# Attention parts made two chunks ahead, and the second head's softmax one step behind the first's

## The chip, the cores and the metric

The kernel runs on one core of a Trainium2 chip. The metric is the device time of one execution in microseconds (us). The core has a matrix engine (TensorE, PE in the profile; its weight loads are PEld), a vector engine (VectorE, DVE), a scalar engine (ScalarE, ACT), a general engine (GpSimd, POOL) and a queue that issues most transfers (SyncE, SP). Each works through its own instructions in order and waits for the others by semaphores.

## The reference

A trunk of two layers over 256 tokens and 2048 features, in float32. The first layer mixes tokens by a gated MLP, the second by attention with a forget gate; each is followed by a convolutional feed-forward part. The change lies in the second layer's attention: 16 heads of 128 features, two blocks of 128 queries, the second of which sees all 256 keys.

```python
def forgetting_attention(xn, w_qg, q_norm, w_out, k, v, c):
    qg = xn @ w_qg
    q, g = jnp.split(qg, 2, axis=-1)
    q = rmsnorm(q.reshape(B, S, N_HEADS, HEAD_DIM), q_norm).transpose(0, 2, 1, 3)
    ...
        s = (jnp.einsum('bhqd,bhkd->bhqk', qb, kb).astype(jnp.float32) * scale
             + c[:, :, lo:hi, None] - c[:, :, None, :hi])
        mask = (lo + jnp.arange(Q_BLOCK))[:, None] >= jnp.arange(hi)[None, :]
        s = jnp.where(mask, s, -jnp.inf)
        p = jax.nn.softmax(s, axis=-1).astype(vb.dtype)
        outs.append(jnp.einsum('bhqk,bhkd->bhqd', p, vb))
    ...
    o = o * jax.nn.sigmoid(g)
    return o @ w_out
```

The keys k, the values v and the sums c of log forget gates come from one shared projection `w_kvf` of the first layer's output.

## The kernel before

**Chunks.** All projections are a single stream of weight chunks (class `Stream`), each 128 x 1024 numbers. For chunk i the loop in `run` issues the load of chunk i+6 on SP (L78, `raw`), splits chunk i+3 into a rounded part on ACT (L112, `whi`) and a remainder on DVE (L113, `wlo`), and then issues chunk i's matmuls (L216): rounded times rounded, rounded times remainder, remainder times rounded. There are four buffers each of `raw`, `whi` and `wlo`. In the values' blocks a chunk is 24 matmuls of 256 columns, and a block of 512 outputs has 8 chunks; in the gate's blocks (`b_g`) there are 4 chunks to a block of 256 outputs.

**Steps.** Everything that is not a weight matmul is written as generators. After each chunk's matmuls `advance` takes every pending generator one step further, to its next `yield`. So a `yield` is a distance of one chunk, and what stands between two of them is issued behind the chunk's matmuls, in the order in which the generators were started. Since ACT and DVE split three chunks ahead, their instructions for a step stand behind the split of the chunk three later.

**Attention.** `heads` is one of these generators. It starts with the first of the 32 chunks of the values (`kvf_v`) and runs on into the gate's chunks. It takes the heads in pairs, a pair every four chunks. A pass of its loop, which this text calls a batch, does this:

- the bias of the next pair's scores from `cB` and `ccol` on ACT (L1205, L1206), its mask on POOL (L1208), the fetch of the next `cB` rows (L1138, a transfer that POOL issues);
- on PE, the outputs of a pair whose weights are ready (`parts_pv`, and L1226), into a tile of the `ps` buffers, and the scores of the next pair (`parts_qk`, and L1229), into the two `mp` buffers;
- a `softmax` started for each of the two heads, and the outputs copied over their queries on ACT (L1233).

A product of the batch with 256 columns is made of parts as the weights' are: `query_parts` rounds queries and keys on ACT (L1166, L1167) and makes the remainders on DVE (L1169, L1170) a step later; `weight_parts` does the same for values and softmax weights (L1180, L1181, then L1185, L1188). There is one tile of parts for each of the two kinds, so they can be overwritten only when the batch before has read them.

`softmax` takes a head's scores from its `mp` buffer (L1147 on DVE, with the maximum in L1149), then exponentiates on ACT (L1152), then normalises and transposes on DVE (L1154, L1156, L953), a step each. `exchange` writes the transposed weights to memory in four transfers on SP (L960), and reads them back two steps later in another layout (L964). A step after that they are in `waiting`, from which `weight_parts` takes them.

Where `heads` starts, `head_norm` of the last block of keys still has work on DVE (L1048, L953). `between` lets the next weight matmuls run 512 columns wide. The buffers `ps` (three), `mp` (two), `big` (six) and `turned` (two) are given out as they come free.

Of the kernel before, what the change touches and what calls it, by code (L numbers as in the profile page):

```python
# [23 lines left out]
NH = 16  # L24
# [154 lines left out]
def build(ctx, tc, d, out):  # L179
# [25 lines left out]
    def main_ps():  # L205
        return psum.tile([P, 2, 512], F32, name="ps", tag="ps", bufs=3)

    def misc_ps():
        return psum.tile([P, 512], F32, name="mp", tag="mp", bufs=2)
# [5 lines left out]
    def mm(o, a, b, start, stop):  # L215
        nc.tensor.matmul(o, a, b, start=start, stop=stop, skip_group_check=True)  # L216

    def between():


        state["wide"] = [8, 2]
# [720 lines left out]
    def att(key):  # L942
        ph.open("att")
        shape = {"X2": [P, KD, 2 * T], "q": [P, NH, T], "k": [P, 4, 8, 4, 32], "v": [P, 2, D],
                 "ccol": [P, 2, NH], "gain": [P, 1]}[key]
        return ph.keep(key, shape, F32R if key == "X2" else F32)

    def blocks_turned(src):


        n = src.shape[1]
        turned = ph.temp("turned", [P, 512], bufs=1 if ph.name == "ffn1" else 2)[:, :n * P].rearrange("p (c h j) -> p c h j", c=4, h=n)
        nc.vector.transpose(turned.rearrange("p c h j -> p h c j"), src.rearrange("p h (c i) -> p h c i", c=4))  # L953
        return turned.rearrange("p c h j -> p c (h j)")
# [11 lines left out]
    def exchange(key, turned, new, then):  # L966

        way = rows_out(key, turned)
        yield
        yield  # L970
        dst = new()
        rows_in(dst, way)
        yield
        then(dst)
# [26 lines left out]
    def part_places(which):  # L1001

        side.open("parts")
        return [side.keep(f"{which}{n}", [P, 2, 2, n], F32R) for n in (P, T)]
# [56 lines left out]
    def four_rows(n):  # L1061
        return ph.temp("rows", [P, 512], bufs=6)[:, :n * P].rearrange("p (r x) -> p r x", r=4)
# [66 lines left out]
    def heads():  # L1129

        assert state["kept"]
        q, k, v, ccol = att("q"), att("k"), att("v"), att("ccol")
        rows, waiting, ready = {}, [], []
        (qp, kp), (vp, pp) = part_places("qk"), part_places("pv")

        def fetch(hd):
            rows[hd] = ph.temp("cB", [P, T])
            nc.gpsimd.dma_start(rows[hd], cd[hd:hd + 1, :].to_broadcast([P, T]))  # L1138

        def softmax(hd, S, L):  # L1140
            if hd % 2:
                yield
                yield
            parts = [(0, L[:, :P]), (1, L[:, P:])]
            mx = ph.temp("mx", [P, 2])
            sm = ph.temp("sm", [P, 2])
            nc.vector.scalar_tensor_tensor(L, S, SCALE, L, op0=OP.mult, op1=OP.add)  # L1147
            for tb, l in parts:
                nc.vector.tensor_reduce(mx[:, tb:tb + 1], l, axis=AX.X, op=OP.max, negate=True)  # L1149
            yield  # L1150
            for tb, l in parts:
                nc.scalar.activation(l, l, AF.Exp, bias=mx[:, tb:tb + 1], accum_out=sm[:, tb:tb + 1])  # L1152
            yield
            nc.vector.reciprocal(sm, sm)  # L1154
            for tb, l in parts:
                nc.vector.tensor_scalar(l, l, sm[:, tb:tb + 1], None, op0=OP.mult)  # L1156
            turned = blocks_turned(L.rearrange("p (h x) -> p h x", h=3))
            yield
            yield from exchange(f"p{hd}", turned, lambda: four_rows(3),
                                lambda dst: waiting.append((hd, dst.rearrange("p r (b j) -> p r b j", b=3))))  # L1160

        def query_parts(n):

            qq, kk = q[:, n:n + 2, P:], k[:, n // 4, :, n % 4:n % 4 + 2, :].rearrange("p t h j -> p h t j")
            kv = [kp[:, i].rearrange("p h (t j) -> p h t j", t=8) for i in range(2)]
            nc.scalar.activation(qp[:, 0], qq, AF.Copy)  # L1166
            nc.scalar.activation(kv[0], kk, AF.Copy)  # L1167
            yield
            nc.vector.tensor_tensor(qp[:, 1], qq, qp[:, 0].bitcast(F32), op=OP.subtract)  # L1169
            nc.vector.tensor_tensor(kv[1], kk, kv[0].bitcast(F32), op=OP.subtract)  # L1170

        def weight_parts():

            take = [hd for hd, _ in waiting if hd < state["v"]][:2]
            for hd in take:
                pT = waiting.pop(0)[1]
                i = hd % 2
                assert all(i != x % 2 for x, _ in ready)
                ready.append((hd, pT))
                nc.scalar.activation(vp[:, 0, i], v[:, 0, hd * P:(hd + 1) * P], AF.Copy)  # L1180
                nc.scalar.activation(pp[:, 0, i].rearrange("p (b r j) -> p r b j", b=2, r=4), pT[:, :, :2, :], AF.Copy)  # L1181
            yield
            for hd, pT in ready[len(ready) - len(take):]:
                i = hd % 2
                nc.vector.tensor_tensor(vp[:, 1, i], v[:, 0, hd * P:(hd + 1) * P], vp[:, 0, i].bitcast(F32),  # L1185
                                        op=OP.subtract)
                hi, lo = (pp[:, l, i].rearrange("p (b r j) -> p r b j", b=2, r=4) for l in range(2))
                nc.vector.tensor_tensor(lo, pT[:, :, :2, :], hi.bitcast(F32), op=OP.subtract)  # L1188

        def three(o, stat, mov, start, stop):  # L1190
            for j, (x, y) in enumerate(((0, 0), (0, 1), (1, 0))):
                mm(o, stat[:, x], mov[:, y], start and j == 0, stop and j == 2)

        for hd in range(2):
            fetch(hd)
        yield
        yield from query_parts(0)
        yield
        n = 0
        while state["done"] < NH:  # L1200
            pair = {hd: ph.temp("big", [P, 512], bufs=6)[:, :3 * P] for hd in (n, n + 1)} if n < NH else {}
            for hd, L in pair.items():
                cB = rows.pop(hd)
                l = L.rearrange("p (a b) -> p a b", a=3)
                nc.scalar.activation(l[:, 0, :], cB[:, :P], AF.Identity, scale=-1.0, bias=ccol[:, 0, hd:hd + 1])  # L1205
                nc.scalar.activation(l[:, 1:, :], cB.rearrange("p (a b) -> p a b", a=2), AF.Identity, scale=-1.0,  # L1206
                                     bias=ccol[:, 1, hd:hd + 1])
                nc.gpsimd.affine_select(l[:, 0::2, :], l[:, 0::2, :], pattern=[[0, 2], [-1, P]],  # L1208
                                        compare_op=OP.is_ge, fill=NEG, base=0, channel_multiplier=1)
                if hd + 2 < NH:  # L1210
                    fetch(hd + 2)
            if not pair and len(ready) < min(2, NH - state["done"]):
                yield from weight_parts()
                yield
                continue
            go, ready[:] = ready[:], []
            if go or pair:
                between()
            o = main_ps()[:, 0, :] if go else None
            S = {hd: misc_ps()[:, :3 * P] for hd in pair}  # L1220
            for i, (hd, pT) in enumerate(go):
                three(o[:, i * T:(i + 1) * T], vp[:, :, hd % 2], pp[:, :, hd % 2], i == 0, False)
            for hd in pair:
                three(S[hd][:, P:], qp[:, :, hd % 2], kp[:, :, hd % 2], True, False)
            for i, (hd, pT) in enumerate(go):
                nc.tensor.matmul(o[:, i * T + P:(i + 1) * T], v[:, 1, hd * P:(hd + 1) * P], pT[:, :, 2, :],  # L1226
                                 start=False, stop=True, skip_group_check=True)
            for hd, L in pair.items():
                nc.tensor.matmul(S[hd][:, :P], q[:, hd, :P], k[:, hd // 4, :4, hd % 4, :], start=False, stop=True,  # L1229
                                 skip_group_check=True)  # L1230
                s.start(softmax(hd, S[hd], L))
            for i, (hd, pT) in enumerate(go):
                nc.scalar.activation(q[:, hd, :], o[:, i * T:(i + 1) * T], AF.Copy)  # L1233
                state["done"] += 1
            yield
            if n + 2 < NH:
                yield from query_parts(n + 2)
            else:
                yield
            yield from weight_parts()  # L1240
            yield
            n += 2
        s.start(taken_back())
# [144 lines left out]
```

## Time and profile before

| | |
|---|---|
| median of 3 runs | 2169.18 us (2169.12 to 2170.85) |
| profiled execution | 2172.16 us, span 2170.4 us |
| PE busy | 2156.1 us, 99% of the span |
| DVE busy | 1648.4 us, 76% |
| ACT busy | 1212.9 us, 56% |
| granted TensorE clock, mean | 0.998 |
| first to last start of a score product of the batches | 1174.7 to 1273.0 us |

A row of the timeline gives start, duration, engine, line and operation, then output<-inputs; what follows in square brackets is the idle time of the engine ahead of it and what ended it. `att_big` is a `big` tile (here the scores), `att_X` the keys' and values' operand. In the stretches of the span, each engine's busy time is followed by its number of instructions, and the column after POOL is the granted clock as a share of full speed.

### The profile page before, as it was taken

The page shows a single profiled execution, that of the slowest core. Times are in us where ns is not written, and L with a number is a line of the kernel's source. Part 1 is how long each engine was busy: PE and PEld are TensorE (multiplying, and loading weights), DVE is VectorE, ACT ScalarE, POOL GpSimd, SP SyncE. Part 2 cuts the span into 40 slices and gives each one's busy share as a digit, 9 for nine tenths or more (in the row PEclk, how much of TensorE's full clock was granted, in tenths as well). Part 3 has the DMA queues.
Part 4 walks back from the last instruction along what each step waited for, and adds up shares of the span by engine and source line. Part 5 has one row for each costly group of instructions (what it writes and reads, how often), then busy time and mean ns, then how long its engine had stood idle before and what let it go on. Part 6 is the DMA issues. An engine that isn't in the chain of part 4 may idle for free.

```text
span 2170.4 us, 45367 instructions
## 1 busy us (share of the span) xinstructions
PE 2156.1 (99%) x18572; PEld 2138.7 (99%) x18572; DVE 1648.4 (76%) x2410; ACT 1212.9 (56%) x1692; POOL 25.4 (1%) x46
## 2 busy tenths in 40 slices
PE   9999999999999999999999999999999999999998
PEld 9999999999999999999999999999999999999998
DVE  6696687777777699976777886677877777779997
ACT  6665555555555555554545775455555555555555
POOL 0000000000000000000001100000000000000000
PEclk9999999999999999999999999999999999999999
DMA  8686566666666567776787877666866666666665
GB/s 310 189 242 206 193 198 194 191 197 190 198 193 195 178 201 224 225 227 193 250 251 257 237 220 236 194 215 190 270 194 194 192 197 191 197 192 186 205 204 165
DMA packets 159858, 454.68 MB, mean 209 GB/s; under 512 B 26321, under 2 KB 48609, under 8 KB 159265
## 3 DMA queue, kind: packets, MB, share of 16 engines
q1 hardware_dynamic: 158112, 447.82, 66.2%
q0 software_dynamic: 1072, 3.41, 0.6%
q8 instruction: 145, 2.38, 0.4%
q10 hardware_dynamic: 464, 0.55, 0.1%
q14 instruction: 65, 0.52, 0.1%
HBM read 434.39 MB, written 17.32 MB: 208 GB/s over the span
## 4 chain that ended last, share of the span: by engine, by line
PE 91%; DVE 4%; DMA 3%; issue 1%; ACT 1%; SPq 1%; DVEq 0%; POOL 0%; ACTq 0%; POOLq 0%
PE ps L216 89%; DVE wlo L113 2%; PE mp L216 1%; DMA way_h<-ffn_turned 1%; DMA raw<-kvf_v 1%; DMA raw<-kvf_k 1%; SPq L960 0%; ACT whi L112 0%; DVE att_big L1048 0%; DVE ffn_turned L953 0%; PE mp L780 0%; DMA way_k<-att_turned 0%; DMA raw<-b_g 0%; DMA raw<-kvf_fk 0%; PE mp L1229 0%
## 5 line engine op out<-in xcount | busy, mean ns | idle before, releaser
L113 DVE TENSOR_TENSOR wlo<-raw,whi 128x1024 fp32r<-128x1024 f32 (+1 forms) x732 | 888.1, 1219 | 282.4 <-ACT whi L112 278.0
L112 ACT ACTIVATE whi<-raw 128x1024 fp32r<-128x1024 f32 (+1 forms) x732 | 769.8, 1058 | 579.5 <-PE ps L216 451.8
L216 PE MATMUL ps<-X,whi 128*128 128x256 f32 (+1 forms) x6466 | 823.6, 280 | 0.0
L216 PEld LDWEIGHTS ps<-X,whi 128*128 128x128 f32 x6466 | 775.3, 188 | 6.8
L216 PE MATMUL ps<-X,wlo 128*128 128x256 f32 x3328 | 445.3, 276 | 0.2 <-DVE wlo L113 0.2
L216 PEld LDWEIGHTS ps<-X,wlo 128*128 128x128 f32 x3328 | 409.8, 188 | 2.1 <-DVE wlo L113 0.4
L216 PE MATMUL ps<-whi,ffn_H 128*128 128x256 f32 (+1 forms) x1852 | 303.1, 277 | 0.0
L216 PEld LDWEIGHTS ps<-whi,ffn_H 128*128 128x128 f32 x1852 | 255.5, 188 | 0.7
L216 PE MATMUL ps<-whi,X 128*128 128x256 f32 (+1 forms) x1336 | 221.9, 279 | 0.0
L216 PE MATMUL ps<-wlo,ffn_H 128*128 128x256 f32 (+1 forms) x924 | 192.3, 277 | 0.0
L216 PEld LDWEIGHTS ps<-whi,X 128*128 128x128 f32 x1336 | 187.7, 188 | 1.5
L924 DVE SCALAR_TENSOR_TENSOR ffn_room<-ffn_room,col 128x255 f32<-128x255 f32 x352 | 161.9, 481 | 6.4
L216 PE MATMUL ps<-whi,att_X 128*128 128x256 f32 (+2 forms) x970 | 164.3, 285 | 0.0
L216 PEld LDWEIGHTS ps<-wlo,ffn_H 128*128 128x128 f32 x924 | 144.4, 188 | 0.2
L216 PE MATMUL ps<-wlo,X 128*128 128x256 f32 (+1 forms) x666 | 144.4, 279 | 0.0
L216 PEld LDWEIGHTS ps<-whi,att_X 128*128 128x128 f32 x970 | 135.9, 188 | 3.4
L392 DVE TENSOR_TENSOR ffn_room<-ps,rB 128x512 f32<-128x512 f32 x76 | 52.5, 691 | 112.8 <-PE ps L216 112.8
L920 ACT ACTIVATE ffn_room<-ffn_room,col 128x256 f32<-128x256 f32 x176 | 96.3, 595 | 52.9 <-DVE ffn_room L392 52.9
L216 PEld LDWEIGHTS ps<-wlo,X 128*128 128x128 f32 x666 | 106.4, 188 | 0.4
L216 PE MATMUL ps<-wlo,att_X 128*128 128x256 f32 (+2 forms) x476 | 106.0, 287 | 0.0
L216 PEld LDWEIGHTS ps<-wlo,att_X 128*128 128x128 f32 x476 | 75.7, 188 | 1.1 <-DVE wlo L113 0.2
L90 ACT ACTIVATE whi<-raw 128x768 fp32r<-128x768 f32 x46 | 39.0, 848 | 65.0 <-PE ps L216 48.9
(229 smaller groups left out, 1696.1 us busy)
## 6 DMA issues: line engine op xcount, KB each, us to landing
raw<-up SPq DMA_DIRECT2D x352, 512.0 KB, 4.1
raw<-down SPq DMA_DIRECT2D x154, 512.0 KB, 4.3
raw<-a_in_u SPq DMA_DIRECT2D x32, 512.0 KB, 4.5
raw<-a_out SPq DMA_DIRECT2D x32, 512.0 KB, 4.0
raw<-b_q SPq DMA_DIRECT2D x32, 512.0 KB, 4.7
raw<-kvf_v SPq DMA_DIRECT2D x32, 512.0 KB, 4.6
raw<-b_g SPq DMA_DIRECT2D x32, 512.0 KB, 4.5
raw<-b_out SPq DMA_DIRECT2D x32, 512.0 KB, 4.3
```

Source lines behind the costliest of these rows:

```text
L90: self.nc.scalar.activation(hi[:, cols], src[:, cols], AF.Copy)
L112: self.nc.scalar.activation(h, raw, AF.Copy)
L113: self.nc.vector.tensor_tensor(l, raw, h.bitcast(F32), op=OP.subtract)
L216: nc.tensor.matmul(o, a, b, start=start, stop=stop, skip_group_check=True)
L392: nc.vector.tensor_tensor(a, src, rB[:, None, :].to_broadcast([P, 2, T]), op=OP.mult)
L920: nc.scalar.activation(c[:, m, :], a[:, m, :], AF.Identity, scale=w[2], bias=column(C_CONVB + l * 2 * KF + f))
L924: nc.vector.scalar_tensor_tensor(c[:, m, n:], a[:, m, :T - n], w[k], c[:, m, n:], op0=OP.mult, op1=OP.add)
```

## The change

```diff
@@ -1140,7 +1140,6 @@
         def softmax(hd, S, L):
             if hd % 2:
                 yield
-                yield
             parts = [(0, L[:, :P]), (1, L[:, P:])]
@@ -1193,9 +1192,9 @@
         for hd in range(2):
             fetch(hd)
-        yield
         yield from query_parts(0)
-        yield
+        for _ in range(3):
+            yield
         n = 0
@@ -1232,12 +1231,9 @@
             for i, (hd, pT) in enumerate(go):
                 nc.scalar.activation(q[:, hd, :], o[:, i * T:(i + 1) * T], AF.Copy)
                 state["done"] += 1
-            yield
-            if n + 2 < NH:
-                yield from query_parts(n + 2)
-            else:
-                yield
-            yield from weight_parts()
+            for step in (query_parts(n + 2) if n + 2 < NH else [None], weight_parts()):
+                yield from step
+            yield
             yield
             n += 2
```

Before, with the batch at step 0 of a pair: query copies at 1, query remainders and weight copies at 2, weight remainders at 3, next batch at 4; the first head's softmax takes the scores at 1, the second's at 3. Now: query copies at 0, behind the batch; query remainders and weight copies at 1, weight remainders at 2, next batch at 4; the softmaxes take the scores at 1 and 2. Ahead of the loop the first pair's copies come at step 0 instead of 1, its remainders at 1 instead of 2, and the first batch at step 4 instead of 3. A pair still takes four steps, so counted from the stream's chunks every batch stands one chunk later.

From L1144 to the copies at L1233 line numbers are one lower in the changed kernel, behind the loop four lower.

ACT where `heads` starts (`L112` splits weights, `parts_qk` are the parts of queries and keys, `L1205` starts the first batch's bias). Before:

```order
L112 ACTIVATE whi<-raw 128x1024 x3
L1166 ACTIVATE parts_qk_14603<-att_q 128x256
L1167 ACTIVATE parts_qk_14604<-att_k 128x512
L112 ACTIVATE whi<-raw 128x1024 x2
L1205 ACTIVATE att_big<-att_cB,att_ccol 128x128
L1206 ACTIVATE att_big<-att_cB,att_ccol 128x256
```

Now:

```order
L112 ACTIVATE whi<-raw 128x1024 x2
L1165 ACTIVATE parts_qk_14603<-att_q 128x256
L1166 ACTIVATE parts_qk_14604<-att_k 128x512
L112 ACTIVATE whi<-raw 128x1024 x4
L1204 ACTIVATE att_big<-att_cB,att_ccol 128x128
L1205 ACTIVATE att_big<-att_cB,att_ccol 128x256
```

The first pair's copies stand one chunk earlier, and four splits instead of two lie between them and the first batch.

DVE where `heads` starts (`L1048` and `L953` are `head_norm` of the last keys). Before:

```order
L113 TENSOR_TENSOR wlo<-raw,whi 128x1024
L1048 TENSOR_TENSOR att_big<-ps,att_hr 128x512
L953 STREAM_TRANSPOSE att_turned<-att_big 128x4x4x32
L1169 TENSOR_TENSOR parts_qk_14603<-att_q,parts_qk_14603 128x256
L1170 TENSOR_TENSOR parts_qk_14604<-att_k,parts_qk_14604 128x512
L113 TENSOR_TENSOR wlo<-raw,whi 128x1024 x2
L1147 SCALAR_TENSOR_TENSOR att_big<-mp,att_big 128x384
```

Now:

```order
L1168 TENSOR_TENSOR parts_qk_14603<-att_q,parts_qk_14603 128x256
L1169 TENSOR_TENSOR parts_qk_14604<-att_k,parts_qk_14604 128x512
L113 TENSOR_TENSOR wlo<-raw,whi 128x1024
L1048 TENSOR_TENSOR att_big<-ps,att_hr 128x512
L953 STREAM_TRANSPOSE att_turned<-att_big 128x4x4x32
L113 TENSOR_TENSOR wlo<-raw,whi 128x1024 x3
```

The first pair's remainders, which stood behind the second of the two L1048 with its transpose, now stand ahead of it and of a split.

DVE in a later batch, from the second head's weight remainders on. Before:

```order
L1185 TENSOR_TENSOR parts_pv_14605<-att_v,parts_pv_14605 128x128
L1188 TENSOR_TENSOR parts_pv_14606<-att_rows,parts_pv_14606 128x4x2x32
L1154 RECIPROCAL att_sm<-att_sm 128x2
L1156 TENSOR_SCALAR att_big<-att_big,att_sm 128x128
L1156 TENSOR_SCALAR att_big<-att_big,att_sm 128x256
L953 STREAM_TRANSPOSE att_turned<-att_big 128x3x4x32
L1147 SCALAR_TENSOR_TENSOR att_big<-mp,att_big 128x384
L1149 TENSOR_REDUCE att_mx<-att_big 128x1 x2
L113 TENSOR_TENSOR wlo<-raw,whi 128x1024 x2
```

Now:

```order
L1184 TENSOR_TENSOR parts_pv_14605<-att_v,parts_pv_14605 128x128
L1187 TENSOR_TENSOR parts_pv_14606<-att_rows,parts_pv_14606 128x4x2x32
L1146 SCALAR_TENSOR_TENSOR att_big<-mp,att_big 128x384
L1148 TENSOR_REDUCE att_mx<-att_big 128x1 x2
L113 TENSOR_TENSOR wlo<-raw,whi 128x1024
L1153 RECIPROCAL att_sm<-att_sm 128x2
L1155 TENSOR_SCALAR att_big<-att_big,att_sm 128x128
L1155 TENSOR_SCALAR att_big<-att_big,att_sm 128x256
L953 STREAM_TRANSPOSE att_turned<-att_big 128x3x4x32
```

The second head's scores are taken right behind the weights' remainders, and the first head's normalising and transpose stand a split later.

## Prediction

> **What bounds the kernel now.** I read the page first, then the waits of TensorE, then the timeline at each of them. The page's busy row:
>
> ```profile
> span 2170.4 us, 45367 instructions
> PE 2156.1 (99%) x18572; PEld 2138.7 (99%) x18572; DVE 1648.4 (76%) x2410; ACT 1212.9 (56%) x1692; POOL 25.4 (1%) x46
> ...
> raw<-kvf_v SPq DMA_DIRECT2D x32, 512.0 KB, 4.6
> ```
>
> PE is the bound over nearly the whole span, and the change removes no matmul. It can win only where PE stands still. All waits of PE (total, times, longest):
>
> ```profile
> PE mp L216 <- DVE parts_qk L1170: 2.5, 1, 2.5
> PE mp L216 <- DVE att_big L1147: 2.2, 2, 1.1
> PE mp L780 <- POOL ident L1273: 1.5, 1, 1.5
> PE ps L216 <- DVE wlo L113: 0.2, 1, 0.2
> ```
>
> The first two rows are the attention batches, the others are elsewhere. The first, in the timeline of all engines (start, duration, engine):
>
> ```profile
> 1172.74 0.68 DVE L1048 TENSOR_TENSOR att_big<-ps,att_hr 128x512 f32<-128x512 f32 x1
> ...
> 1174.09 1.18 DVE L113 TENSOR_TENSOR wlo<-raw,whi 128x1024 fp32r<-128x1024 f32 x1
> ...
> 1174.76 0.28 PE L216 MATMUL mp<-parts_qk,parts_qk 128*128 128x256 f32 x1
> ...
> 1175.19 0.68 DVE L1048 TENSOR_TENSOR att_big<-ps,att_hr 128x512 f32<-128x512 f32 x1
> 1175.91 0.71 DVE L953 STREAM_TRANSPOSE att_turned<-att_big 128x512 f32<-128x512 f32 x1
> 1176.55 0.38 DVE L1169 TENSOR_TENSOR parts_qk<-att_q,parts_qk 128x256 fp32r<-128x256 f32 x1
> 1176.85 0.68 DVE L1170 TENSOR_TENSOR parts_qk<-att_k,parts_qk 128x512 fp32r<-128x512 f32 x1
> 1177.45 2.35 DVE L113 TENSOR_TENSOR wlo<-raw,whi 128x1024 fp32r<-128x1024 f32 x2
> 1177.59 1.43 PE L216 MATMUL mp<-parts_qk,parts_qk 128*128 128x256 f32 x5 [2.54 <-DVE parts_qk L1170]
> 1178.89 0.42 ACT L1166 ACTIVATE parts_qk<-att_q 128x256 fp32r<-128x256 f32 x1 [2.87 <-PE mp L216]
> ```
>
> PE reaches the first batch, issues one product with the rounded parts, and idles 2.54 us until DVE, still busy with the last block of k (L1048, L953), has made the remainders. Behind that stands a second loss. Stretches of the span (length, busy time of PE, PEld, DVE, ACT, POOL, granted clock):
>
> ```profile
> 1177.32:1180.73 3.41, 3.15 (x12) 2.95 (x13) 3.38 (x6) 0.94 (x2) 0.00 (x0) 0.50 0.76 200
> 1191.30:1203.40 12.10, 12.10 (x98) 11.64 (x97) 9.54 (x21) 9.20 (x21) 2.91 (x6) 1.00 0.79 222
> 1230.00:1245.00 15.00, 13.88 (x110) 13.35 (x110) 12.80 (x28) 9.76 (x24) 2.69 (x6) 1.00 0.81 245
> ```
>
> For 3.41 us after the wait the granted clock is 0.50; PE is busy for 3.15 of them, work of 1.58 us at full clock. So the wait costs 2.54 + 1.57 = 4.1 us. The second wait, DVE and PE:
>
> ```profile
> 1225.84 0.42 DVE L1169 TENSOR_TENSOR parts_qk<-att_q,parts_qk 128x256 fp32r<-128x256 f32 x1
> ...
> 1226.78 1.22 DVE L113 TENSOR_TENSOR wlo<-raw,whi 128x1024 fp32r<-128x1024 f32 x1
> 1227.92 0.28 DVE L1185 TENSOR_TENSOR parts_pv<-att_v,parts_pv 128x128 fp32r<-128x128 f32 x1
> ...
> 1228.99 0.16 DVE L1154 RECIPROCAL att_sm<-att_sm 128x2 f32<-128x2 f32 x1
> ...
> 1230.48 0.52 DVE L1147 SCALAR_TENSOR_TENSOR att_big<-mp,att_big 128x384 f32<-128x384 f32 x1
> 1231.04 0.61 DVE L1149 TENSOR_REDUCE att_mx<-att_big 128x1 f32<-128x128 f32 x2
> 1231.57 1.22 DVE L113 TENSOR_TENSOR wlo<-raw,whi 128x1024 fp32r<-128x1024 f32 x1
> ```
> ```profile
> 1231.15 0.60 PE L216 MATMUL mp<-parts_qk,parts_qk 128*128 128x256 f32 x3 [1.12 <-DVE att_big L1147]
> 1259.29 0.60 PE L216 MATMUL mp<-parts_qk,parts_qk 128*128 128x256 f32 x3 [1.12 <-DVE att_big L1147]
> ```
>
> The scores of two heads lie in the two mp buffers, and L1147 of a head frees its buffer for the next batch.
> The one PE waits for is the second head's. It ends at 1231.0, 1.12 us late, because in its chunk DVE has wlo (1.14 from start to start), the weights' remainders (1.07), the first head's normalising and transpose (1.49), and only then L1147 and L1149 (1.09): 4.8 us. What a chunk takes on PE shows in the chain that ended last:
>
> ```profile
> 1191.30 0.72 PE mp L216 x6
> 1192.46 11.00 PE ps L216 x86
> 1203.46 0.72 PE mp L216 x6
> ```
>
> Four chunks are 11.0 us, a chunk 2.75. DVE is uneven over the four chunks of a pair, not short of time: 12.80 busy in the 15.00 us around the wait.
>
> **The change part by part.** No instruction is added or removed. Counted by chunk, the parts stay where they are (only the first pair's, made before the loop, go one earlier); the batch, its bias copies on ACT, its mask and fetch on POOL, and the first head's softmax go one later, so all parts are made two or more chunks ahead, and the second softmax keeps its chunk.
>
> First batch. DVE's remainders now stand after the first L953, ahead of wlo, so from about 1174.2 (L1048 at 1172.74, L953 about 0.7 behind it) to 1175.2. PE does one more chunk first and comes at 1174.65 + 2.75 = 1177.4. Slack 2.2 us: the 2.54 us go, and with the gap the slow stretch. wlo behind the moved pair is about 1.0 us later than 1174.09, for a chunk that starts after the batch, near 1178.6: covered by over 2 us.
>
> Steady batches, from the moment PE ends one. ACT copies the attention out, makes the next query parts, then splits a weight:
>
> ```profile
> 1232.23 0.66 ACT L1233 ACTIVATE att_q<-ps 128x256 f32<-128x256 f32 x2 [3.39 <-PE ps L1226]
> ...
> 1234.60 0.41 ACT L1166 ACTIVATE parts_qk<-att_q 128x256 fp32r<-128x256 f32 x1
> 1234.90 0.62 ACT L1167 ACTIVATE parts_qk<-att_k 128x512 fp32r<-128x512 f32 x1
> 1235.53 1.06 ACT L112 ACTIVATE whi<-raw 128x1024 fp32r<-128x1024 f32 x1
> ```
>
> Query copies 0.93 and whi 1.06: 2.0 us. Then DVE: wlo 1.14, query remainders 0.94, first softmax 1.09, wlo 1.14, weights 1.07, second L1147 and L1149 1.09, which makes 8.5 us after the batch. The next batch comes 11.0 us after it, so the buffer is free 2.5 us early, where it was 1.12 us late. Both waits of 1.12 us go. The normalising that used to stand ahead of it falls in the next chunk, which had the lightest load.
>
> What these covers cost if they are gone: the query copies now stand right behind the batch that reads the same tile, so ACT waits for its last product (it did once, 2.87 us in the row of 1178.89), and whi and wlo queue behind. They serve a chunk that PE starts 8.2 us after the batch; ready at 3.1, they have 5 us to spare.
>
> DMA queues. SP issues the four writes of a head's weights and the reading back in neighbouring chunks instead of every second one:
>
> ```profile
> 1215.06 1.77 SPq L960 DMA_DIRECT2D way_p<-att_turned  x4
> 1217.35 5.46 SPq L78 DMA_DIRECT2D raw<-kvf_v  x2
> 1222.99 0.33 SPq L964 DMA_DIRECT2D att_rows<-way_p  x1
> ```
>
> 1.77 us of issue fit in a chunk beside its one weight load. The second head's transfers keep their chunk and the first head's go one later, which leaves them three chunks, 8.2 us, between the reading back and the copy that needs it. The fetches on POOL go one chunk later with the bias that needs them, and the pool is idle. At the end, the gates read the attention output a chunk later; the last batch is in the fourth block of the gate's eight, and no wait of PE stands there. All cost nothing.
>
> Sum: −2.54 − 1.57 − 2 × 1.12 = −6.35 us. The profiled execution of 2172.16 us (its span and 1.8 us around it) would become 2165.8. The median of the runs is 3.0 us below it; the same sum makes it 2169.18 − 6.35 = **2162.8 us**. The one term whose size a timed run may not have is the slow stretch: 0 to 1.57 us. I take the whole, as the only execution with a clock row shows it.
>
> On that term a page speaks. The Trainium skill, "TensorE: Matmul & The Clock Gate", Part 1 (The HAM clock gate), says the clock falls to half only after at least one idle window of about 3.4 us, in a free-running window of that length. The trace agrees on the half and on 3.41 us, but PE was idle for only 2.54; the measurement decides for the profiled execution. By the page alone the term would be 0 and the sum −4.8.
>
> **The rivals.**
> A (forecast): 2162.8.
> B: the waits go, but the runs that set the median had no slow stretch. For it: the runs spread over 1.73 us (2169.12 to 2170.85), about one stretch. Against: the profiled execution had it. 2169.18 − 4.78 = 2164.4. This is what the page's rule gives.
> C: the wait moves to the second batch. PE arrives 4.1 us earlier while DVE, 3.38 busy of 3.41 us after the first wait, loses that pause. Chaining the durations above with weight loads of 4.6 us, the second head's L1147 would be done some 1.5 us before the second batch; a load late by more than that shows. It costs 0 to 2.5 us, the largest wait in the list: about 2165.3.
> D: nothing gained, since DVE merely passes the same delay on: 2169.2. Against: 12.80 of 15.00 us.
> E, slower: ACT, held by the query copies behind each batch, starves PE of whi. If that cost what the first wait did at all eight batches, 8 × 2.54 = 20.3 us, the time is 2183.1. It decides once copies, whi and wlo take over 8.2 us against 3.1; a load landing 5 us later than 4.6 would do it.
> That the parts do not move earlier is no rival of its own: the batch moving later is the same distance.
>
> **How the numbers follow.** Chances: A 0.40, B 0.26, C 0.18, D 0.11, E 0.05. About 0.2%, 4.3 us, is what a measurement can tell here, so faster means under 2164.8: most of A, over half of B, a little of C, 0.57; slower is E, 0.05; the rest, 0.38, is within. The range runs from 2161.3 (A less most of the spread of the runs) to 2167.5 (C on top of B, 2164.4 + 2.5, and a little), leaving out D and E.
>
> **What would show it.** After: no wait of PE on parts_qk or on the second head's L1147, granted clock 1.00 throughout the attention stage, PE's idle time down by 4.8 us. A wait on wlo or whi after a batch means E; one at the second batch alone means C. I am wrong if DVE or the weight loads prove late by more than the 1.5 to 2.5 us of slack.

## The result, and the profile after

| | before | after |
|---|---|---|
| median of 9 runs each, same chip | 2170.35 us (2168.03 to 2171.67) | 2163.39 us (2163.26 to 2165.08) |
| ratio, 95% interval | | 0.9971 (0.9960 to 0.9981) |
| profiled execution | 2172.16 us | 2163.74 us |

The changed kernel is 7.0 us faster (4.1 to 8.7 by the interval); forecast were 6.35 us, and a time of 2162.8. Its runs also agree better: eight of nine lie within 0.5 us, while those of before spread over 3.6.

The page of the changed kernel, span and busy time, and the first row of the chain that ended last:

```profile
span 2162.0 us, 45349 instructions
PE 2152.6 (100%) x18572; PEld 2136.3 (99%) x18572; DVE 1649.4 (76%) x2410; ACT 1212.8 (56%) x1692; POOL 25.9 (1%) x46
...
PE 99%; DVE 0%; ACT 0%; issue 0%; POOL 0%; DVEq 0%; ACTq 0%; POOLq 0%
```

The busy times of DVE and ACT are those of before to 1.0 us, since the same work is done in another order. All waits of PE that are left:

```profile
PE mp L780 <- POOL ident L1269: 1.5, 1, 1.5
```

The two rows of the attention batches are gone, and none has taken their place. The attention stage in one stretch (length, busy time and instructions of PE, PEld, DVE, ACT and POOL, granted clock, DMA share, GB/s), first before, then after:

```profile
1165.00:1320.00 155.00, 150.21 (x1182) 144.43 (x1181) 123.82 (x240) 105.87 (x228) 18.00 (x30) 0.99 0.76 228
```
```profile
1165.00:1320.00 155.00, 155.00 (x1245) 150.00 (x1244) 130.09 (x245) 110.20 (x233) 17.85 (x30) 1.00 0.78 235
```

PE idled for 4.8 us of the 155 before and is busy throughout now, at a clock of 1.00. The first batch, on DVE and then on PE:

```profile
1171.37 0.68 DVE L1048 TENSOR_TENSOR att_big<-ps,att_hr 128x512 f32<-128x512 f32 x1
...
1172.72 0.38 DVE L1168 TENSOR_TENSOR parts_qk<-att_q,parts_qk 128x256 fp32r<-128x256 f32 x1
1173.03 0.68 DVE L1169 TENSOR_TENSOR parts_qk<-att_k,parts_qk 128x512 fp32r<-128x512 f32 x1
```
```profile
1176.64 0.88 PE L216 MATMUL mp<-parts_qk,parts_qk 128*128 128x256 f32 x6
```

The remainders are done at 1173.7, 2.9 us before PE comes for them. The place where the second wait was is read from the batch of 1214.0. In the chain that ended last (start, duration):

```profile
1214.00 0.72 PE mp L216 x6
1215.61 11.72 PE ps L216 x92
1227.33 0.72 PE mp L216 x6
```

ACT and DVE after it (in brackets the idle time ahead and what ended it):

```profile
1215.20 0.66 ACT L1232 ACTIVATE att_q<-ps 128x256 f32<-128x256 f32 x2 [0.62 <-PE ps L1225]
...
1216.57 1.06 ACT L112 ACTIVATE whi<-raw 128x1024 fp32r<-128x1024 f32 x1
```
```profile
1217.66 1.23 DVE L113 TENSOR_TENSOR wlo<-raw,whi 128x1024 fp32r<-128x1024 f32 x1 [1.73 <-ACT whi L112]
...
1219.74 0.55 DVE L1146 SCALAR_TENSOR_TENSOR att_big<-mp,att_big 128x384 f32<-128x384 f32 x1
...
1223.07 0.55 DVE L1146 SCALAR_TENSOR_TENSOR att_big<-mp,att_big 128x384 f32<-128x384 f32 x1
```

The second L1146 is the second head's. It ends at 1223.6, 8.0 us after the weight matmuls behind the batch began at 1215.6, and PE comes back to that buffer at 1227.33: 3.7 us early, where it was 1.12 us late. No `wlo` or `whi` stands among PE's waits.

Aligned by the same weight matmuls, the two profiled executions part by 8.4 us of span: 4.2 at the first batch, 1.35 at each of the two later waits, 0.2 in smaller steps behind these two, and 1.3 at three places whose code is the same in both (0.35 at the start, 0.5 in the projection of the keys, 0.46 in a feed-forward part near 1530 us). That 1.3 us is not the change's: between the profiled execution of before and that of the kernel with the first gap filled (below), 1.1 us part at the same three places.

### The profile page after: what moved, and what is told of

The parts are those of the page before. It is cut to its first block, busy times and chain, and to the rows that moved or that the text cites. A ratio compares the mean times of both kernels' runs of the same rounds, so it can differ in the third digit from the quotient of the medians.

```text
span 2162.0 us, 45349 instructions
## 1 busy us (share of the span) xinstructions
PE 2152.6 (100%) x18572; PEld 2136.3 (99%) x18572; DVE 1649.4 (76%) x2410; ACT 1212.8 (56%) x1692; POOL 25.9 (1%) x46
## 3 DMA queue, kind: packets, MB, share of 16 engines
q0 software_dynamic: 1072, 3.41, 0.7%
## 4 chain that ended last, share of the span: by engine, by line
PE 99%; DVE 0%; ACT 0%; issue 0%; POOL 0%; DVEq 0%; ACTq 0%; POOLq 0%
PE ps L216 98%; PE mp L216 1%; PE mp L780 0%; PE mp L1228 0%; PE ps L1225 0%; ACT sq L441 0%; DVE h_h L747 0%; DVE h_h L440 0%; DVE h_h L741 0%; PE mp L412 0%; ACT fin_t L733 0%; DVE fin_t L737 0%; DVE h_h L717 0%; DVE fin_y L736 0%; DVE rcol L738 0%
## 5 line engine op out<-in xcount | busy, mean ns | idle before, releaser
L112 ACT ACTIVATE whi<-raw 128x1024 fp32r<-128x1024 f32 (+1 forms) x732 | 770.0, 1057 | 570.0 <-PE ps L216 448.5
```

The source lines that it names most:

```text
L112: self.nc.scalar.activation(h, raw, AF.Copy)
```

## The experiments

The forecast was that the later waits went because the second softmax no longer stands behind the first head's normalising. Call this theory 1, the order on DVE. The trace of before offers another reason. A finished block of values is copied out of `ps` by ACT (L1075, in `v_evict`, two activations). Blocks have eight chunks and batches come every four, so every second batch shared its chunk with such a copy. ACT before, after the batch of 1245, and DVE's first split after the batches of 1217, 1231 and 1245:

```profile
1245.69 0.66 ACT L1233 ACTIVATE att_q<-ps 128x256 f32<-128x256 f32 x2 [2.30 <-PE ps L1226]
...
1247.11 1.26 ACT L1075 ACTIVATE att_v<-ps,rcol 128x512 f32<-128x512 f32 x2
1248.25 1.07 ACT L112 ACTIVATE whi<-raw 128x1024 fp32r<-128x1024 f32 x1
```
```profile
1221.20 1.23 DVE L113 TENSOR_TENSOR wlo<-raw,whi 128x1024 fp32r<-128x1024 f32 x1 [3.88 <-ACT whi L112]
...
1234.73 1.23 DVE L113 TENSOR_TENSOR wlo<-raw,whi 128x1024 fp32r<-128x1024 f32 x1 [1.95 <-ACT whi L112]
...
1249.35 1.23 DVE L113 TENSOR_TENSOR wlo<-raw,whi 128x1024 fp32r<-128x1024 f32 x1 [3.10 <-ACT whi L112]
```

After a batch with a copy DVE stands idle for 3.10 us (3.88 after the batch of 1217), as `whi` stands behind the 1.26 us of the copy on ACT; after one without it, 1.95. Both waits of before, at 1231 and 1259, come four chunks behind a batch with a copy; the batch of 1245, four chunks behind one without, has none. With the change the batch stands a chunk later and the copy has a chunk of its own (it starts at 1211.00, three microseconds ahead of the batch). Call this theory 2, where the batch stands against the blocks. All times below are medians against runs of the kernel before on the same chip: 2169.98 us (28 runs) for the first four, 2170.25 for the others (28 runs on one chip, 21 on another, with the same median). Each list of waits is that of one profiled execution.

**Only the softmax.** The second head's softmax follows by one step; all else as before.

```diff
             if hd % 2:
                 yield
-                yield
```

> The kernel before, with one yield instead of two ahead of the second head's softmax; parts, batches and prologue stay. Theory 1 (the order on DVE: the second head's scores are read behind a normalising and a transpose): L1146 of the second head moves a chunk ahead, so both waits of 1.12 us on it go; the first batch's wait of 2.54 us on the query remainders and the stretch at clock 0.50 behind it stay: about 2.5 us faster than before. Theory 2 (the copy of a finished block of values, L1075 on ACT, falls in the chunk of a batch and holds up whi, so DVE starts late): the copy still shares the batch's chunk, so the waits stay, 0 us.

2167.31 us (2165.92 to 2168.31, 11 runs), ratio 0.9990 (0.9981 to 0.9998), so 2.7 us less. PE's waits in the attention:

```profile
PE mp L216 <- DVE parts_qk L1169: 2.0, 1, 2.0
```

The later waits are gone though the copy still shares the chunk: the order alone is enough to remove them. The first wait stays.

**Only what stands ahead of the loop.** Loop and softmax as before.

```diff
-        yield
         yield from query_parts(0)
-        yield
+        for _ in range(3):
+            yield
```

> The kernel before, with the changed prologue alone: the first pair's parts one step earlier, the first batch one step later, so every batch stands one chunk later; the loop and the softmax keep their old steps. Theory 1 (order on DVE): the first wait and the slow stretch go, 4.1 us, and the two waits of 1.12 us on the second head's L1147 stay, as the load of the chunk ahead of a batch is unchanged. Theory 2 (the copy of values on ACT collides with the batch): batches now stand behind the first chunk of a block, the copy behind the last, so all three waits go: 6.4 us faster, like the full change.

2163.87 us (2163.23 to 2164.88, 9 runs), ratio 0.9974 (0.9965 to 0.9984). The only wait of PE left is that of L780. The later waits go although the second softmax stands where it stood: theory 2's place is enough too, and these lines bring what the whole change does, as far as the runs can tell.

**Only the copy moved.** The copy of a block comes a step later, out of the batch's chunk; all else as before.

```diff
         def done(ps):
+            yield
             v = att("v")
```

> The kernel before, with only the copy of a finished block of values out of PSUM (L1075 before, two ACT copies of 0.68 us) put off by one step, so that it no longer shares a chunk with a batch. Theory 1 (order on DVE): the chunk ahead of a batch still holds 4.8 us of DVE work, the waits of 1.12 us stay: 0 us. Theory 2 (collision on ACT): both waits of 1.12 us go, the first wait stays: about 2.5 us faster.

2168.45 us (2166.94 to 2170.02, 11 runs), ratio 0.9993 (0.9984 to 1.0002). PE's waits in the attention:

```profile
PE mp L216 <- DVE parts_qk L1171: 3.0, 1, 3.0
```

DVE's idle time after the batch of 1217 falls from 3.88 us to 2.73, and the later waits go, as theory 2 has it. The time does not show it clearly. The first wait of the profile grew from 2.54 to 2.98 us: PE came 0.71 us sooner (1174.05 against 1174.76), the remainders only 0.29 sooner. With the lines ahead of the loop unchanged, this gap differs from profile to profile, from 1.84 to 2.98 us (below).

**The changed kernel with the batch on the block's end.** The first batch at step 3, so that batch and copy share a chunk again.

```diff
-        for _ in range(3):
+        for _ in range(2):
             yield
```

> The changed kernel, with the first batch at step 3 instead of 4: every batch stands where it stood before, behind the last chunk of a block, and shares its chunk with the copy of values on ACT; the parts are two chunks ahead and the second softmax one step behind. Theory 1 (order on DVE): no wait on the second head's scores; the first pair's remainders end about when PE arrives (1173.7 against 1173.9 in the trace of the changed kernel), so at most 0.5 us of wait there and no slow stretch: within 0.5 us of the changed kernel. Theory 2 (collision on ACT): two waits of about 1 us come back, 2 to 2.5 us slower than the changed kernel.

2163.67 us (2162.97 to 2164.77, 8 runs), ratio 0.9972 (0.9962 to 0.9983), and no wait in the attention. With the new order the shared chunk costs nothing, as theory 1 has it. The first pair's remainders are done at 1174.06, and PE comes at 1174.43.

**One step more ahead of the loop.** The kernel before, its first batch at step 4 instead of 3.

```diff
         yield from query_parts(0)
         yield
+        yield
```

> The kernel before, with only the first batch one step later; the first pair's parts stay at steps 1 and 2, loop and softmax as before. The remainders end near 1177.5 us, PE comes at 1177.4: the first wait shrinks to 0.2 us or less, with no slow stretch; all batches leave the chunk of the copy of values, so the steady waits go too: about 6 us faster, like the full change. If the first wait stays above 1 us, PE's arrival is not what sets it.

2164.03 us (2163.66 to 2165.03, 6 runs), ratio 0.9968 (0.9956 to 0.9980), no wait in the attention. One `yield` gives what can be measured of the whole change: it gives the remainders of the first batch a chunk more and takes all later batches off the copies.

**The copy put back into the batch's chunk.** The same, with the copy a step later as well.

```diff
         def done(ps):
+            yield
             v = att("v")
 ...
         yield from query_parts(0)
         yield
+        yield
```

> The kernel with only the first batch one step later (which had no wait left), and the copy of a finished block of values put off by one step, so that it shares a chunk with a batch again. Theory 2 (the collision on ACT together with the late second softmax makes the steady waits): two waits of 0.7 to 1.2 us on the second head's scores come back, 1.6 to 2.7 us slower than without the delay of the copy. Rival (it was the batch's place behind the last chunk of a block, whatever ACT copies there): no wait, the same time.

2166.82 us (2165.99 to 2167.98, 11 runs), ratio 0.9985 (0.9976 to 0.9993): 2.8 us over the last one. PE's waits, then ACT and DVE after the batch of 1214:

```profile
PE mp L216 <- DVE att_big L1148: 2.2, 2, 1.1
```
```profile
1215.61 0.66 ACT L1235 ACTIVATE att_q<-ps 128x256 f32<-128x256 f32 x2 [2.15 <-PE ps L1228]
...
1217.04 1.26 ACT L1076 ACTIVATE att_v<-ps,rcol 128x512 f32<-128x512 f32 x2
1218.17 1.07 ACT L112 ACTIVATE whi<-raw 128x1024 fp32r<-128x1024 f32 x1
```
```profile
1219.28 1.23 DVE L113 TENSOR_TENSOR wlo<-raw,whi 128x1024 fp32r<-128x1024 f32 x1 [3.88 <-ACT whi L112]
```

Both waits return with the copy, at the old size, and DVE's idle time of 3.88 us with them.

**The changed kernel's loop and softmax, with the old lines ahead of the loop.**

```diff
+        yield
         yield from query_parts(0)
-        for _ in range(3):
-            yield
+        yield
```

> The changed kernel with the old prologue: the parts in the loop a step earlier and the second softmax one step behind, but the first pair's parts at steps 1 and 2 and the first batch at step 3. Theory: the prologue alone carries the first wait, so 2 to 3 us of wait on the first pair's remainders and a stretch at clock 0.50 stay, and the steady waits go by the order on DVE, as with the softmax edit alone: about 2167.3, 2.7 us faster than before. Rival (the loop's parts bring something of their own): 2166 or less.

2166.80 us (2165.67 to 2168.50, 11 runs), ratio 0.9985 (0.9976 to 0.9994), one wait:

```profile
PE mp L216 <- DVE parts_qk L1169: 1.8, 1, 1.8
```

That is 3.4 us less than before, against 2.7 with the softmax alone. The intervals overlap, so that the loop's earlier parts bring something of their own is neither shown nor excluded. That its profile would show a slow stretch was a miss: the clock is 1.00 there, though five of its eleven runs list a mean clock of 0.998 and may have had one.

**The changed kernel without the softmax's edit.**

```diff
             if hd % 2:
                 yield
+                yield
```

> The changed kernel with the second head's softmax two steps behind again, as before. Its weights then come back one step after the parts are taken, so weight parts take one head fewer the first time and the heads run one batch longer (nine batches with outputs instead of eight). No collision with the copy of values and the first pair early: no wait of PE, and the time of the changed kernel plus 0 to 0.5 us for the additional batch, so the softmax edit is worth at most that here. If order on DVE alone decided, waits of 0 to 0.5 us per batch would show.

2168.65 us (2167.31 to 2169.87, 10 runs), ratio 0.9991 (0.9982 to 1.0000). A miss: some 5 us over the changed kernel, where 0 to 0.5 were expected. PE's waits:

```profile
PE mp L216 <- DVE att_big L1147: 2.9, 5, 0.8
```

The old softmax is late at five batches, though the batches stand clear of the copies, as in the changed kernel. The earlier loop is therefore safe only together with the earlier softmax, and the two edits of the change cannot be taken apart at will. Aligned by the same weight matmuls, its profile and the changed kernel's part by 4.6 us: 0.3 ahead of the attention, some 4.0 at the five batches with a wait, and 0.3 for the additional batch (1320.1), which makes the output of one head that the first batch with outputs then lacks.

**The first gap filled.** The kernel before, with 24 matmuls of 256 columns, whose result nothing reads, ahead of the first batch: PE is busy in the gap, which stays as long.

```diff
+            if n == 0:
+                spare, x = main_ps()[:, 0, :T], att("X2")[:, 0, :]
+                for _ in range(24):
+                    mm(spare, x[:, :P], x[:, :T], True, True)
```

> The kernel before, with 24 additional matmuls of 256 columns (0.113 us each in the trace, 2.7 us together) into a spare PSUM tile that nothing reads, ahead of the first batch, so that PE works where it idled; the first pair's parts come no earlier. Theory 1 (the half clock follows from PE's idling): the wait is filled, the clock stays at 1.00, and the kernel is 1.4 to 1.7 us faster although it does more work. Rival (the half clock comes from something else at that place, or only the wait costs): a stretch at 0.50 stays, and the time is that of the kernel before or up to 0.7 us longer.

2169.50 us (2168.90 to 2170.44, 11 runs), ratio 0.9995 (0.9987 to 1.0004). The slow stretch is gone (clock 1.00 throughout the attention); in its profile the first batch ends 1.4 us sooner against the stream than before. The runs are 0.75 us faster, with an interval that includes none: less than the 1.4 to 1.7 expected. The filling was too long in this profile: the remainders are done at 1176.21, and PE gets to the score products at 1176.99. So the 0.75 is likely too small a price for the stretch.

**The first pair's parts a step earlier, the batch left where it was.**

```diff
         for hd in range(2):
             fetch(hd)
-        yield
         yield from query_parts(0)
         yield
+        yield
```

> The kernel before, with only the first pair's query parts one step earlier; the first batch stays at step 3, loop and softmax as before. The remainders should end near 1173.7 us, where PE comes at about 1174: the first wait and the slow stretch go (4.1 us, up to 0.5 us less if PE comes first). The batches still share their chunk with the copy of values, and the second head's scores are still read late, so by both theories together two waits of about 1.1 us stay: 2166 against 2170. If the steady waits go too, the backlog of the first batch was their cause and not the copy.

2166.35 us (2165.46 to 2168.68, 11 runs), ratio 0.9984 (0.9975 to 0.9993). PE's waits in the attention's batches:

```profile
PE mp L216 <- DVE att_big L1147: 2.2, 2, 1.1
PE mp L216 <- DVE parts_qk L1170: 1.3, 1, 1.3
```

The later waits stay, as they must. The first is halved in this profile and not removed, against an expected 0.5 at most. But the kernel with the batch on the block's end has the same lines ahead of its loop and no such wait, and the execution profiled here (2168.29 us) is among the three slowest of its eleven. So the parts' step earlier was enough in one of these two profiles and not in the other; the batch's step later was enough in the profile that has it without the parts' (one step more).

## Why the prediction was right, and where its reasons fell short

The time came out at 2163.39 us where 2162.8 was forecast. Part of that closeness is luck: the forecast started from 2169.18, the median of three runs, where nine gave 2170.35, and of its two terms the first was likely too large and the second too small.

**First batch, 4.1 us: right in the profile, likely too large for the runs.** The profiled executions give 4.2. The remainders were forecast for 1175.2 and came at 1173.7; PE, forecast for 1177.4, came at 1176.6. (The execution after was 0.84 us ahead of that before at this place, so PE came as forecast and the remainders 0.7 us sooner.)

The gap's 2.54 us are those of one execution: three other profiles with the same lines ahead of the loop have 1.84, 2.04 and 2.98. The slow stretch's 1.57 is what rival B disputed. Each run lists its mean granted clock, and half speed for 3.41 us takes 3.41 × 0.5 / 2170 = 0.0008 from it, which is about the last digit shown. Of the 77 runs of before beside the experiments, 47 show 0.998 or less; of the 75 runs of the changed kernel and of those experiments whose first gap is gone, filled or halved, all show 0.999. So the kernel before ran into the slow stretch in at least some six of ten executions (at least, since the digit is coarse: one profile that has the stretch reads 0.999). Its 45 runs at 0.998 average 0.7 us more than the 30 at 0.999 (interval 0.25 to 1.10), and filling the gap gained 0.75. By the runs the whole first batch is worth 3.4 us (the copy put back, which has the two later waits alone, against before), 0.7 less than forecast. Its interval, 1.5 to 5.2, does not exclude 4.1, so that "I take the whole" was too much is likely and not shown.

**Later waits, 2 × 1.12 us: the size was low.** The aligned traces give 1.35 each, and the runs 2.67 for both with the softmax alone and 2.79 with the return of the copy. PE's idle time before the products was the floor of the price, not the whole of it.

**Why they go: half the cause.** The prediction's DVE chain, 8.5 us after a batch, was near the 8.0 measured, and its slack of 2.5 us was 3.7. But it read the lateness from the order on DVE alone, and said that the parts' place was all that moved by the batch's extra chunk. That its chain still fitted was luck in part: it was read after the batch of 1231, which has no copy, and applied to all. The wait needs two things at once, by one profile of each kernel:

| | old softmax order | new softmax order |
|---|---|---|
| copy in the batch's chunk | two waits of 1.1 us (before, copy put back, gap filled, parts early) | none (softmax alone, loop and softmax, batch on the block's end) |
| copy in another chunk | none (ahead of the loop only, one step more, copy moved) | none (the changed kernel) |

This holds for the loop as it was, and for the new loop with the new softmax; the new loop with the old softmax has its own five waits. The row of DVE idle for 3.88 us ahead of `wlo` is in the trace of before, and the prediction did not use it. After the first block's copy (1191.85) no wait followed. DVE has no remainders of weights to make yet there (no row of L1185 stands between 1188 and 1204), which would explain it; no run tests that.

**Rivals.** C did not show: no wait at the second batch. D did not: the median fell. E did not: behind the query copies `whi` starts at 1216.57, 1.4 us after the batch's last copies began, and no wait of PE names it.

**A rule of the Trainium skill.** By the Trainium skill, "TensorE: Matmul & The Clock Gate", Part 1, the clock falls only after an idle window of about 3.4 us. The traces do not agree: gaps of 2.04, 2.54 and 2.98 us were each followed by a stretch at half speed. What it would make of the time, no stretch at all, holds for at most some four in ten of the runs of before.

## What to carry to other kernels

When a buffer comes free late, follow the late engine's idle time upstream before its work: here DVE looked crowded, but it had been idle for 3.9 us behind ACT, 1.2 of them for a copy that the code places elsewhere (2.73 us were left with the copy moved). Where two periodic jobs meet every second period, moving one by a step can be worth as much as reordering either; try the smallest shift alone first. And a term that depends on the clock is to be sized from the clocks of many runs, not from one profile.

## What the runs showed of the hardware

Not expected: gaps of PE far shorter than 3.4 us can be followed by half speed, and a difference of 0.2 us in the gap can go with having it or not. The first score products behind the gap and the next weight matmuls, with the softmax alone (gap 2.04 us):

```profile
1176.05 0.86 PE L216 MATMUL mp<-parts_qk,parts_qk 128*128 128x256 f32 x5 [2.04 <-DVE parts_qk L1169]
...
1177.12 0.77 PE L216 MATMUL ps<-whi,att_X 128*128 128x512 f32 x1
```

and with loop and softmax (gap 1.84 us), at full speed:

```profile
1175.95 0.85 PE L216 MATMUL mp<-parts_qk,parts_qk 128*128 128x256 f32 x5 [1.84 <-DVE parts_qk L1169]
...
1177.00 0.48 PE L216 MATMUL ps<-whi,att_X 128*128 128x512 f32 x1
```

With the softmax alone the slow stretch again lasts 3.41 us at a clock of 0.50. It starts a microsecond after the gap's end; before the change it started (1177.32) ahead of the gap's end (1177.59). The stretch with the softmax alone:

```profile
1177.10:1180.51 3.41, 3.41 (x11) 2.73 (x10) 2.25 (x5) 0.72 (x2) 0.00 (x0) 0.50 0.98 299
```

Gaps of 2.54 and 2.98 us had the stretch in their profiles, one of 1.25 had not. The length of the gap is not all that counts. In each of the twelve traces the clock first rises 5 to 8 us after the start and then stays at 1.00 for a whole number of 3.413 us: for 343 of them (1170.77 us) in the three that have the slow stretch, for 630 to 632 in the others, which first fall to 0.50 at the kernel's end. So in these traces the clock changed only at the edges of fixed windows of 3.41 us. What PE did in the window that holds most of the gap, before the change and with loop and softmax:

```profile
1173.91:1177.32 3.41, 1.13 (x10) 0.93 (x9) 3.38 (x6) 1.84 (x4) 2.91 (x4) 1.00 0.86 239
```
```profile
1174.42:1177.83 3.41, 1.88 (x13) 1.74 (x14) 2.61 (x4) 1.06 (x3) 0.91 (x2) 1.00 0.63 142
```

PE was busy for 1.13 us of that window before the change, 1.37 with the softmax alone and 1.03 with the copy moved, and the next window ran at half speed. With 1.88 (loop and softmax) and 2.17 (first parts early) it did not. Where between 1.37 and 1.88 us the limit lies, and whether there is one, these few windows do not show. That a gap can fall into one window or across two would explain why the same kernel has the stretch in some executions and not in others.
